# Head-pair statistics reloaded at step 6 and used from step 12, next-head loads asked for at step 6 of every other head

## The chip, the core and the metric

The kernel runs on one core of one Trainium2 chip. The core has a matrix engine (PE, with its weight loads counted apart as PEld), a vector engine (DVE), an activation engine (ACT), a general engine (POOL) and a sync engine (SP). Tiles live in SBUF, matrix results in PSUM, and larger arrays in DRAM. Copies between DRAM and SBUF are DMAs. Three engines issue them here, each into a queue of its own: SP (queue q1 in the profile), ACT (q10) and POOL (q0). All three queues are served by the same 16 DMA engines.

The metric is device time in microseconds (us) of one launch. The kernel before took 2467.77 us as the median of three runs (2467.73 to 2468.74).

## The reference

One decoder layer over 2048 tokens of width 1024, all in float32. The part that matters here is the attention of 8 heads of width 64. Every head has dilated windows; the kernel computes them as a *near* window (dilation 1) and a *far* one (dilations 4 and 16 together), and joins the two by their row maxima and softmax denominators:

```python
w = d * jnp.exp(m - jnp.max(m, axis=0, keepdims=True))
w = w / jnp.sum(w, axis=0, keepdims=True)
return jnp.sum(w[..., None] * o, axis=0)
```

Before the attention a projection makes queries, keys, values and a pooling branch; behind it come the output projection, a gated MLP with a causal convolution, a gate with per-layer embeddings, and a last RMS norm.

## The kernel before, in words

The program has three phases in a row: `phase_project` (to about 400 us in the trace), `phase_attention` (about 400 to 722 us) and `phase_rest` (the remaining 1740 us). The change touches only `phase_attention`.

**Steps.** A head's 2048 queries are cut into 16 chunks of 128. The loop `for s in range(NS + 10)` runs over 128 steps, 16 for each of 8 heads, and in each step calls the stages listed in `CFG["ord"]`, each for the step `s` minus its lag. A step computes near and far scores (lines 572, 573, 561, 562 on PE), adds the position bias and takes the row extreme (577 and 583 on DVE), exponentiates (589 and 593 on ACT), transposes the result (600, PE), copies it as a high and a low part (613 ACT, 617 DVE), and multiplies by the values (628 and 642, PE). Two of four steps end with `ev<-o` (659, ACT) and `s<-o,ev` (660, DVE), which fold a group of four chunks into the tiles `s1` (near) and `s3` (far). PE, ACT, DVE and POOL run in the order in which this loop writes their instructions (`manual_schedule`). SP is not in that list: the framework's scheduler places its DMAs, so the step at which the loop asks for a load need not be the place at which it stands in SP's queue.

**Loads.** `load_qk(h)` asks for eight tiles of a head: `qhh`, `ks`, `qll` for each half of the partitions (512 KB each), the far bias `fb` (256 KB) and the near bias `nb` (128 KB). Every tag has one buffer for even heads and one for odd heads, so a head's tiles can come in as soon as the head two before it is through. `load_v` brings value tiles (`v`, 512 KB), eight for a pair of heads. All these are DMAs of SP (line 56).

**Statistics of a pair.** Two heads form a pair; pairs are counted 0 to 3 and heads 0 to 7. When pair `pr` is done, its row extremes and denominators (`st1`, `st3`) go through five transposes (764, 767) into `sx` and `sy`. Let `d` be the step counted from the start of the next pair, so that d = 0 is the first step of heads 2, 4 and 6. The stage `M` (`mix`) then does:

- d = 1: `mix_stats_store` writes `sx` and `sy` to DRAM (`std`, `stf`; DMAs of ACT, lines 776 and 777).
- d = 4: `mix_stats_load` reads them back, turned, as `sn` and `sf` (DMAs of ACT, lines 784 and 788; 32 KB each in runs of 16 numbers, 64 bytes).
- d = 9: `mix_lift` takes the smaller extreme and the exponents (862, 865, 866 on DVE, 867 on ACT).
- d = 10: `mix_weights` makes the weights (874 to 879, DVE), and POOL writes them to DRAM (`wd`, 880).
- d = 13 + 4c for c = 0 to 3: `mix_fetch` (891, POOL) brings the weights of 512 tokens back, spread over partitions (`wb`); d = 19 + 4c: `mix_products` (901, 902, 908, POOL); d = 20 + 4c: `mix_store` (913, 914, 924, 925, POOL).

Pair 3 has no next pair and is joined in another way (`last_near`, `last_far`, `last_weights`), which the change doesn't touch.

**Waits of the DMAs.** The built program gives the DMAs of SP and ACT eight completion counters in turn (`DMAHW0` to `DMAHW7` in its listing). A DMA waits until the one before it on its counter has landed, whatever that moved. The engine that issues it waits too, and so does all that stands behind it on that engine.

Of the kernel before, what the change touches and what calls it, by code (L numbers as in the profile page):

```python
# [20 lines left out]
S = 2048  # L21
H = 8
# [18 lines left out]
V_N = V_CB + 2 * NF  # L41


CFG = {"tt": 2, "ee": 2, 'ord': [['B', 0], ['M', 0], ['N', 0], ['S', 1], ['o', 7], ['F', 0], ['h', 2], ['nm', 0], ['p', 7], ['fm', 0], ['l', 2], ['T', 1], ['V', 6], ['W', 6], ['ne', 0], ['fe', 0]], 'perm': [3, 2, 1, 0], 'fp': [[0], [1], [2], [3]], 'np': [[0, -1], [1], [2], [3]], 'm': [9, 10, 13, 4, 6, 7]}


class Shared:
# [7 lines left out]
def rdma(nc, dst, src):  # L55
    nc.sync.dma_start(fp(dst) if dst.dtype == F32R else dst, fp(src) if src.dtype == F32R else src)
# [429 lines left out]
def phase_attention(tc, g, mx, near_b, far_b):  # L486
# [5 lines left out]
    with ExitStack() as ctx:  # L492
# [42 lines left out]
        def begin(s):  # L535
# [7 lines left out]
            st = steps[s] = Shared()  # L543
            st.n = n = n - n % 4 + CFG["perm"][n % 4]
            st.t, st.pt, st.e = heads[h], pairs[h // 2], h % 2
# [5 lines left out]
            st.d1, st.d3 = st.pt.st1[:, 1, st.e, n : n + 1], st.pt.st3[:, st.r, 1, st.e, st.i : st.i + 1]  # L551
            st.tt = sb.tile([P, 768], F32, tag="tt", bufs=CFG["tt"], name="tt")
            st.ee = sb.tile([P, 768], F32, tag="ee", bufs=CFG["ee"], name="ee")

# [64 lines left out]
        def near_pv(gi, kbs, first):  # L619
            gr, q0 = groups[gi], 4 * (gi % 4)  # L620
            for kb in kbs:
                if q0 + kb < 0:
                    continue
                m0, m1 = max(0, kb), min(3, kb + 1)
                b0, b1 = 4 * m0 + kb + 1, 4 * m1 + kb + 1
                kt = q0 + kb
                for pt in (gr.h, gr.l):
                    nc.tensor.matmul(
                        gr.o[:, m0 * P : (m1 + 1) * P],
                        vals[gi // 8, "v1", kt // 4][:, kt % 4, gi // 4 % 2, :],  # L630
                        pt[:, b0 : b1 + 1 : 4, :],
                        start=first,
                        stop=False,
                        skip_group_check=True,
                    )
                    first = False

        def far_pv(gi, kbs, first):
            gr = groups[gi]
            for kb in kbs:  # L640
                for pt in (gr.h, gr.l):
                    nc.tensor.matmul(
                        gr.o[:, kb * P :],
                        vals[gi // 8, "v3", gi % 4][:, kb, gi // 4 % 2, :],
                        pt[:, 6 * kb + 2 : 18 + kb : 5, :],
                        start=first,
                        stop=False,
                        skip_group_check=True,
                    )
                    first = False  # L650
# [11 lines left out]
        def values(v):  # L662
# [4 lines left out]
            if part < 2:  # L667
                far_pv(gi, CFG["fp"][2 * part], part == 0)
            else:
                near_pv(gi, CFG["np"][2 * part - 4], part == 2)  # L670

        def values_b(v):
            gi, part = v // 4, v % 4
            if part < 2:
                far_pv(gi, CFG["fp"][2 * part + 1], False)
            else:
# [28 lines left out]
        def mix(s):  # L705
            for pr in range(NPAIR - 1):
                d = s - (pr + 1) * 2 * NQ
                if d == 1:
                    mix_stats_store(nc, g, pr, pairs[pr])
                if d == 4:  # L710
                    mix_stats_load(nc, g, mx, pr, pairs[pr])
                if d == CFG["m"][0]:
                    mix_lift(nc, g, mx, pairs[pr])
                if d == CFG["m"][1]:
                    mix_weights(nc, g, mx, pr, pairs[pr])
                for c in range(NCH):
                    if d == CFG["m"][2] + CFG["m"][3] * c:
                        mix_fetch(nc, g, mx, nc.gpsimd, pr, pairs[pr], c)
                    if d == CFG["m"][2] + CFG["m"][3] * c + CFG["m"][4]:
                        mix_products(nc, g, mx, nc.gpsimd, pairs[pr], c)  # L720
                    if d == CFG["m"][2] + CFG["m"][3] * c + CFG["m"][5]:
                        mix_store(nc, g, mx, nc.gpsimd, nc.gpsimd, pr, pairs[pr], c)()
# [5 lines left out]
        with tc.manual_schedule(engines=set(EN.values())):  # L728
            for dst, src in load_qk(0):
                rdma(nc, dst, src)  # L730
            for q in range(4):
                for which in ("v3", "v1"):
                    rdma(nc, *load_v(0, which, q))
            queue = []
            stages = {
                "F": far_scores, "N": near_scores, "fm": far_max, "nm": near_max, "fe": far_exp, "ne": near_exp,
                "T": turn, "h": high, "l": low, "V": values, "W": values_b, "S": stats, "M": mix, "o": fold, "p": folded, "B": begin
            }
            for s in range(NS + 10):
                if s < NS:  # L740
                    h, n = divmod(s, NQ)
                    if n == 1 and h + 1 < H:
                        queue += load_qk(h + 1)
                    if queue:
                        rdma(nc, *queue.pop(0))
                    for pr in range(1, NPAIR):
                        if s - 2 * NQ * (pr - 1) in V_STEPS:
                            rdma(nc, *load_v(pr, *V_STEPS[s - 2 * NQ * (pr - 1)]))
                if s == NS + 2:
                    last_far(nc, g, mx, ps_t, pairs[NPAIR - 1])  # L750
                    pieces = pairs[NPAIR - 1].pieces = last_weights(nc, mx, pairs[NPAIR - 1])
                for nm, lag in CFG["ord"]:
                    if 0 <= s - lag < NS or nm == "M":
                        stages[nm](s - lag)
                for _ in range({NS + 3: 3, NS + 4: 2, NS + 5: 1}.get(s, 0)):
                    next(pieces)
# [18 lines left out]
def mix_stats_store(nc, g, pr, pt):  # L775
    nc.scalar.dma_start(g.std[pr], pt.sx)
    nc.scalar.dma_start(g.stf[pr], pt.sy)


def mix_stats_load(nc, g, sb, pr, pt):  # L780
    q = nc.scalar
    pt.sn = sb.tile([P, 2, 2, 16], F32, tag="sn", name="sn")
    pt.sf = sb.tile([P, 2, 2, 16], F32, tag="sf", name="sf")
    q.dma_start(
        pt.sn.rearrange("p a e r -> p (a e) r"),
        g.std[pr].rearrange("(ae n) q -> ae (n q)", n=NQ).rearrange("ae (i r) -> i ae r", r=16),
    )
    q.dma_start(
        pt.sf.rearrange("p a e r -> p (a e) r"),
        g.stf[pr].rearrange("(ae n) q -> ae (n q)", n=4).rearrange("ae (i r) -> i ae r", r=16),  # L790
    )
# [66 lines left out]
def mix_lift(nc, g, sb, pt):  # L858

    sn, st3 = pt.sn, pt.sf  # L860
    lo = sb.tile([P, 2, 16], F32, tag="lo", name="lo")
    nc.vector.tensor_tensor(lo, sn[:, 0], st3[:, 0], op=ALU.min)
    pt.wts = sb.tile([P, 2, 2, 16], F32, tag="wts", name="wts")
    ex = sb.tile([P, 2, 2, 16], F32, tag="ex", name="ex")
    nc.vector.tensor_tensor(ex[:, 0], lo, sn[:, 0], op=ALU.subtract)
    nc.vector.tensor_tensor(ex[:, 1], lo, st3[:, 0], op=ALU.subtract)
    nc.scalar.activation(pt.wts, ex, AF.Exp)


def mix_weights(nc, g, sb, pr, pt):  # L870

    sn, st3, wts = pt.sn, pt.sf, pt.wts
    dn = sb.tile([P, 2, 2, 16], F32, tag="dn", name="dn")
    nc.vector.tensor_tensor(dn[:, 0], wts[:, 0], sn[:, 1], op=ALU.mult)
    nc.vector.tensor_tensor(dn[:, 1], wts[:, 1], st3[:, 1], op=ALU.mult)
    nc.vector.tensor_tensor(dn[:, 0], dn[:, 0], dn[:, 1], op=ALU.add)
    rs = sb.tile([P, 2, 16], F32, tag="rs", name="rs")
    nc.vector.reciprocal(rs, dn[:, 0])
    nc.vector.tensor_tensor(wts, wts, rs[:, None, :, :].to_broadcast([P, 2, 2, 16]), op=ALU.mult)
    nc.gpsimd.dma_start(  # L880
        g.wd[pr].rearrange("ae (i r) -> i ae r", r=16), wts.rearrange("p a e r -> p (a e) r")
    )


def mix_fetch(nc, g, sb, q, pr, pt, c, bufs=2):

    cs = slice(c * CH, (c + 1) * CH)
    wb = []
    for a in range(2):
        w = sb.tile([P, CH], F32, tag=f"wb{a}", bufs=bufs, name=f"wb{a}")  # L890
        q.dma_start(w, g.wd[pr][2 * a : 2 * a + 2, None, cs].to_broadcast([2, DH, CH]))
        wb.append(w)
    pt.__dict__.setdefault("wb", {})[c] = wb
# [1078 lines left out]
```

## Time and profile before

The profiled execution took 2463.29 us; its span from the first to the last instruction is 2461.2 us. All rows quoted from the trace come from this one execution.

| | |
|---|---|
| median of the runs | 2467.77 us (3 runs) |
| profiled execution | 2463.29 us, span 2461.2 us |
| mean granted PE clock | 0.982 |
| DMA moved | 476.06 MB, mean 193 GB/s |
| DMA of the SP queue | 396.21 MB, 51.3% of 16 engines' span |
| DMA of the ACT queue | 27.77 MB, 3.2% |

How to read it: the *timeline* lists instructions with their start, their duration, and in brackets how long the engine had been idle before and what ended that. "SPq" and "ACTq" rows are DMA issues, which cost the issuing engine little; the transfer itself lands later. The *windows* give, for a stretch of time, how long each engine was busy, the granted PE clock (1.00 is full), the mean busy share of the DMA engines and what they moved. The *chain* is the work that ended last, followed back; each piece shows its start, its length and what it was. The *DMA issues* give the size and the median time from issue to landing.

### The profile page before, as it was taken

The page shows a single profiled execution, that of the slowest core. Times are in us where ns is not written, and L with a number is a line of the kernel's source. Part 1 is how long each engine was busy: PE and PEld are TensorE (multiplying, and loading weights), DVE is VectorE, ACT ScalarE, POOL GpSimd, SP SyncE. Part 2 cuts the span into 40 slices and gives each one's busy share as a digit, 9 for nine tenths or more (in the row PEclk, how much of TensorE's full clock was granted, in tenths as well). Part 3 has the DMA queues.
Part 4 walks back from the last instruction along what each step waited for, and adds up shares of the span by engine and source line. Part 5 has one row for each costly group of instructions (what it writes and reads, how often), then busy time and mean ns, then how long its engine had stood idle before and what let it go on. Part 6 is the DMA issues. An engine that isn't in the chain of part 4 may idle for free.

```text
span 2461.2 us, 32489 instructions
## 1 busy us (share of the span) xinstructions
PE 2345.0 (95%) x11251; PEld 1969.5 (80%) x11251; DVE 1723.8 (70%) x2705; ACT 1147.7 (47%) x2055; POOL 528.9 (21%) x515
## 2 busy tenths in 40 slices
PE   8999999887878999999999999999989999999998
PEld 7888887786766887888888788788878888888888
DVE  6645427686875266999999999877766565755655
ACT  5423326786861134444445545444444444543332
POOL 3312221043350023334432366100000000000100
PEclk9999999898989999999999999999999999999999
DMA  7535348777737585456566787544378786654332
GB/s 239 175 132 184 146 156 248 174 171 175 197 124 269 187 265 194 158 192 202 192 206 212 265 278 273 201 139 139 129 251 310 222 260 203 221 176 154 126 102 90
DMA packets 250564, 476.06 MB, mean 193 GB/s; under 512 B 47744, under 2 KB 74176, under 8 KB 247328
## 3 DMA queue, kind: packets, MB, share of 16 engines
q1 hardware_dynamic: 204704, 396.21, 51.3%
q0 software_dynamic: 26048, 50.00, 6.0%
q10 hardware_dynamic: 19648, 27.77, 3.2%
q8 instruction: 88, 1.44, 0.2%
q14 instruction: 76, 0.62, 0.1%
HBM read 313.08 MB, written 160.73 MB: 193 GB/s over the span
## 4 chain that ended last, share of the span: by engine, by line
PE 73%; DVE 10%; DMA 8%; issue 3%; ACT 2%; POOL 0%; SPq 0%; DVEq 0%; POOLq 0%; ACTq 0%
PE ua L1319 15%; PE uc L1319 7%; PE dn L90 5%; PE dn L89 5%; PE dn L91 5%; PE ub L1319 4%; PE z L91 4%; PE z L89 4%; PE z L90 4%; PE o L91 2%; PE o L89 2%; PE o L90 2%; PE gp L89 2%; PE gp L90 2%; PE gp L91 2%
## 5 line engine op out<-in xcount | busy, mean ns | idle before, releaser
L89 PE MATMUL dn<-ah,wu 128*128 128x512 f32 x616 | 240.8, 391 | 5.3 <-ACT ah L84 5.3
L90 PE MATMUL dn<-al,wu 128*128 128x512 f32 x616 | 240.6, 391 | 2.1 <-DVE al L85 2.0
L91 PE MATMUL dn<-ah,wu 128*128 128x512 f32 x616 | 240.2, 390 | 0.0
L85 DVE TENSOR_TENSOR al<-ra,ah 128x512 fp32r<-128x512 f32 x154 | 105.9, 690 | 109.0 <-ACT ah L84 108.8
L89 PE MATMUL z<-hnh,wh 128*128 128x512 f32 (+1 forms) x480 | 170.1, 354 | 9.3 <-ACT hnh L252 5.8
L90 PE MATMUL z<-hnl,wh 128*128 128x512 f32 (+1 forms) x480 | 169.8, 354 | 3.6 <-DVE hnl L253 3.5
L91 PE MATMUL z<-hnh,wl 128*128 128x512 f32 (+1 forms) x480 | 169.7, 354 | 2.3 <-POOL wl L85 1.7
L84 ACT CAST ah<-ra 128x512 fp32r<-128x512 f32 x154 | 95.2, 621 | 143.1 <-PE dn L91 133.9
L110 POOL TENSOR_TENSOR pw<-ms,mhalf 128x4 f32<-128x4 f32 (+1 forms) x18 | 17.9, 995 | 636.3 <-ACT ms L108 636.3
L89 PEld LDWEIGHTS dn<-ah,wu 128*128 128x128 f32 x616 | 115.9, 188 | 30.3 <-ACT ah L84 6.2
L90 PEld LDWEIGHTS dn<-al,wu 128*128 128x128 f32 x616 | 116.0, 188 | 27.1 <-DVE al L85 3.2
L91 PEld LDWEIGHTS dn<-ah,wu 128*128 128x128 f32 x616 | 116.0, 188 | 24.2
L85 DVE TENSOR_TENSOR wu<-ru,wu 128x1024 fp32r<-128x1024 f32 x88 | 133.4, 1516 | 1.8 <-ACT wu L84 1.8
L1319 PE MATMUL uc<-a22h,wu 128*128 128x512 f32 x352 | 115.8, 390 | 2.4 <-DVE uv L1342 2.4
L1319 PE MATMUL ub<-a12h,wu 128*128 128x512 f32 x352 | 116.8, 392 | 1.2 <-ACT a12h L1375 1.2
L1319 PE MATMUL ua<-s2h,wu 128*128 128x512 f32 x352 | 116.2, 391 | 1.8 <-ACT ug L1520 1.6
L85 DVE TENSOR_TENSOR wu<-rw,wu 128x512 fp32r<-128x512 f32 x149 | 101.1, 688 | 23.5 <-ACT wu L84 23.4
L1319 PE MATMUL ua<-s1h,wu 128*128 128x512 f32 x352 | 115.6, 389 | 0.8 <-ACT ug L1546 0.8
L1319 PE MATMUL ua<-s4h,wu 128*128 128x512 f32 x352 | 115.7, 389 | 0.6 <-ACT uv L1567 0.6
L1319 PE MATMUL uc<-s3h,wu 128*128 128x512 f32 x352 | 115.6, 389 | 0.0
L1319 PE MATMUL ua<-a11h,wu 128*128 128x512 f32 x352 | 115.5, 389 | 0.0
L89 PEld LDWEIGHTS z<-hnh,wh 128*128 128x128 f32 x480 | 94.0, 196 | 21.3 <-ACT hnh L252 5.8
(334 smaller groups left out, 6713.9 us busy)
## 6 DMA issues: line engine op xcount, KB each, us to landing
ru<-in_w_up_dram SPq DMA_DIRECT2D x66, 512.0 KB, 4.2
wr<-in_w_in_dram SPq DMA_DIRECT2D x64, 256.0 KB, 4.2
rw<-in_w_down_dram SPq DMA_DIRECT2D x61, 256.0 KB, 4.0
nt<-h SPq DMA_DIRECT2D x56, 256.0 KB, 4.1
h<-h SPq DMA_DIRECT2D x56, 256.0 KB, 5.2
td<-t SPq DMA_DIRECT2D x22, 512.0 KB, 2.6
t<-td SPq DMA_DIRECT2D x22, 512.0 KB, 3.7
nt<-in_w_down_dram POOLq DMA_DIRECT2D x44, 256.0 KB, 5.1
```

The source lines that it names most:

```text
L84: nc.scalar.copy(hi, src)
L85: (low or nc.gpsimd).tensor_tensor(lo, src, fp(hi), op=ALU.subtract)
L89: nc.tensor.matmul(ps, wh, ah, start=first, stop=False, skip_group_check=again)
L90: nc.tensor.matmul(ps, wh, al, start=False, stop=False, skip_group_check=again)
L91: nc.tensor.matmul(ps, wl, ah, start=False, stop=last, skip_group_check=again)
L110: nc.gpsimd.tensor_tensor(pw[:, :nj], ms[:, :nj], g.mhalf[:, :nj], op=ALU.pow)
L1319: nc.tensor.matmul(pst, x[:, ksl], y, start=first and k == 0 and n == 0, stop=k == HK - 1 and n == 2, skip_group_check=True)
```

## The change

Two edits. The first changes the six numbers `CFG["m"]`, which are read in `mix`: lift at d = 12 (was 9), weights at d = 13 (was 10), fetch at d = 14 + 4c (was 13 + 4c), products five steps behind the fetch (were six) and store six behind it (were seven), so products and stores stay at 19 + 4c and 20 + 4c. With it the load of the statistics moves from d = 4 to d = 6. The second makes even heads (h = 0, 2, 4, 6) ask for the tiles of head h + 1 from their step 6 instead of step 1; odd heads still ask at step 1.

```diff
-... 'm': [9, 10, 13, 4, 6, 7]}
+... 'm': [12, 13, 14, 4, 5, 6]}
...
                 if d == 1:
                     mix_stats_store(nc, g, pr, pairs[pr])
-                if d == 4:
+                if d == 6:
                     mix_stats_load(nc, g, mx, pr, pairs[pr])
                 if d == CFG["m"][0]:
                     mix_lift(nc, g, mx, pairs[pr])
...
                     h, n = divmod(s, NQ)
-                    if n == 1 and h + 1 < H:
+                    if n == (1 if h % 2 else 6) and h + 1 < H:
                         queue += load_qk(h + 1)
```

In the built program ACT's two statistics loads move past two steps of its own work. These are ACT's rows at the start of head 4 (`std_116` and `stf_120` are the statistics of pair 1) before:

```order
L593 ACTIVATE ee,st_5742<-tt,st_5742 128x128 [waits DVE_49]
L784 DMA sn<-std_116 128x4x16 [waits DMAHW6_49,DMAHW2_49]
L788 DMA sf<-stf_120 128x4x16 [waits DMAHW4_49,DMAHW3_49,DMAHW0_49]
L659 COPY ev<-o 64x512 [waits PE_49]
L613 CAST pth<-tp 128x512
```

and in the changed program, from the same row on:

```order
L593 ACTIVATE ee,st_5742<-tt,st_5742 128x128 [waits DVE_49]
L659 COPY ev<-o 64x512 [waits PE_49]
L613 CAST pth<-tp 128x512
L589 ACTIVATE ee,st_5741<-tt,st_5741 128x256 [waits DVE_49,Activation_49]
L593 ACTIVATE ee,st_5742<-tt,st_5742 128x512 [waits DVE_49]
L613 CAST pth<-tp 128x256 [waits PE_49]
L589 ACTIVATE ee,st_5741<-tt,st_5741 128x256 [waits DVE_49,Activation_49]
L593 ACTIVATE ee,st_5742<-tt,st_5742 128x384 [waits DVE_49]
L784 DMA sn<-std_116 128x4x16 [waits DMAHW4_49,DMAHW2_49,DMAHW0_49]
L788 DMA sf<-stf_120 128x4x16 [waits DMAHW6_49,DMAHW3_49]
L659 COPY ev<-o 64x512 [waits PE_49]
```

`DMAHW2` and `DMAHW3` are the stores of `sx` and `sy`, which have to have landed. `DMAHW0` is the value load `v_2_2<-vf` of SP: before, `sf` stood next on its counter, now `sn` does. The other counters named were done long before.

SP's queue at the same place, before (the first number of `qhh`, `ks`, `qll`, `fb`, `nb` is a tile number; these are head 5's tiles, `v_2_...` are values of pair 2):

```order
L56 DMA v_2_2_5821<-vn 128x4x256 [waits DMAHW4_49,PE_49]
L56 DMA qll_5789<-ql_87 64x2048 [waits DMAHW5_49]
L56 DMA qhh_5788<-qh_83 64x2048 [waits DMAHW7_49]
L56 DMA v_2_3_5876<-vf 128x4x256 [waits DMAHW1_49,PE_49]
L56 DMA ks_5790<-kl_95 64x2048 [waits DMAHW2_49]
L56 DMA qll_5789<-ql_87 64x2048 [waits DMAHW3_49]
L56 DMA v_2_3_5934<-vn 128x4x256 [waits DMAHW4_49,PE_49]
L56 DMA fb_5792<-in_far_b_dram 128x512 [waits DMAHW5_49,DVE_49]
L56 DMA nb_5791<-in_near_b_dram 128x256 [waits DMAHW6_49]
```

and in the changed program:

```order
L56 DMA v_2_2_5814<-vn 128x4x256 [waits DMAHW4_49,PE_49]
L56 DMA qll_5920<-ql_87 64x2048 [waits DMAHW5_49]
L56 DMA qhh_5919<-qh_83 64x2048 [waits DMAHW6_49]
L56 DMA v_2_3_5867<-vf 128x4x256 [waits DMAHW7_49,PE_49]
L56 DMA v_2_3_5925<-vn 128x4x256 [waits DMAHW1_49,PE_49]
L56 DMA ks_5921<-kl_95 64x2048 [waits DMAHW3_49]
L56 DMA qll_5920<-ql_87 64x2048 [waits DMAHW4_49]
L56 DMA fb_5923<-in_far_b_dram 128x512 [waits DMAHW5_49,DVE_49]
L56 DMA nb_5922<-in_near_b_dram 128x256 [waits DMAHW6_49]
```

One row has moved: the last value load of the pair stands ahead of two key and query loads instead of behind them. The rest of the order is as it was, but the counters are dealt out anew, since the statistics loads now take theirs two steps later. Before, `nb` waited on the counter of `sn` (`DMAHW6`); now that counter belongs to the second `qhh`, and no load of head 5 waits for `sn` or `sf`.

More of the change, by code (lines that the diff above doesn't have):

```diff
@@ L41 @@
 V_N = V_CB + 2 * NF
-CFG = {"tt": 2, "ee": 2, 'ord': [['B', 0], ['M', 0], ['N', 0], ['S', 1], ['o', 7], ['F', 0], ['h', 2], ['nm', 0], ['p', 7], ['fm', 0], ['l', 2], ['T', 1], ['V', 6], ['W', 6], ['ne', 0], ['fe', 0]], 'perm': [3, 2, 1, 0], 'fp': [[0], [1], [2], [3]], 'np': [[0, -1], [1], [2], [3]], 'm': [9, 10, 13, 4, 6, 7]}
+CFG = {"tt": 2, "ee": 2, 'ord': [['B', 0], ['M', 0], ['N', 0], ['S', 1], ['o', 7], ['F', 0], ['h', 2], ['nm', 0], ['p', 7], ['fm', 0], ['l', 2], ['T', 1], ['V', 6], ['W', 6], ['ne', 0], ['fe', 0]], 'perm': [3, 2, 1, 0], 'fp': [[0], [1], [2], [3]], 'np': [[0, -1], [1], [2], [3]], 'm': [12, 13, 14, 4, 5, 6]}
 class Shared:
```

## The prediction

> **What bounds the kernel now.** I read the page first, then the windows, the waits and the chain inside the attention.
>
> ```profile
> span 2461.2 us, 32489 instructions
> PE 2345.0 (95%) x11251; PEld 1969.5 (80%) x11251; DVE 1723.8 (70%) x2705; ACT 1147.7 (47%) x2055; POOL 528.9 (21%) x515
> ```
>
> PE is busy for 95% of the span, but an average over three phases says little about one of them. The windows below cut the attention into heads 2 to 7, one row each, by the first `tt<-sn,nb` of a head on DVE.
>
> ```profile
> core 0: us, PE busy (x) PEld busy (x) DVE busy (x) ACT busy (x) POOL busy (x), PEclk, DMA share, GB/s
> 474.00:514.10 40.10, 32.40 (x204) 29.68 (x205) 31.47 (x97) 31.30 (x88) 4.11 (x6) 0.96 0.72 167
> 514.10:550.20 36.10, 32.68 (x212) 29.38 (x212) 30.91 (x90) 33.02 (x90) 21.23 (x21) 1.00 0.93 203
> 550.20:601.70 51.50, 35.36 (x204) 32.11 (x205) 31.47 (x98) 31.33 (x88) 16.64 (x19) 0.83 0.76 167
> 601.70:637.80 36.10, 32.67 (x212) 29.33 (x211) 30.93 (x90) 33.01 (x90) 23.28 (x25) 1.00 0.91 215
> 637.80:678.30 40.50, 32.91 (x204) 29.84 (x205) 31.61 (x98) 31.33 (x88) 11.11 (x13) 0.96 0.74 182
> ```
>
> The odd heads 3 and 5 take 36.10 us at full clock; the even heads 2, 4 and 6, in which the statistics of the pair before are handled, take 40.10, 51.50 and 40.50 for nearly the same work on each engine. A head of 16 steps without trouble is thus 36.10 us, **a step 2.26 us** (36.10/16), and the even heads lose 4.0, 15.4 and 4.4 us, together **23.8 us**. That is all that this change can win at the stage where it acts. Where it is lost, the timeline of the longest waits shows (start, duration, instruction, and in brackets the idle time before it with what ended it):
>
> ```profile
> 486.17 0.58 ACT L659 COPY ev<-o 64x512 f32<-64x512 f32 x1 [3.54 <-DMA stf<-sy]
> 487.52 0.58 PE L628 MATMUL o<-pth,v 128*128 128x256 f32 x1 [3.81 <-DVE s L660]
> 564.54 0.58 ACT L659 COPY ev<-o 64x512 f32<-64x512 f32 x1 [5.69 <-DMA v<-vn]
> 565.90 0.58 PE L628 MATMUL o<-pth,v 128*128 128x256 f32 x1 [5.96 <-DVE s L660]
> 584.51 0.19 DVE L862 TENSOR_TENSOR lo<-sn,sf 128x32 f32<-128x32 f32 x1 [7.33 <-DMA sf<-stf]
> 585.43 0.58 PE L572 MATMUL sn<-ks,qhh 128*128 128x256 f32 x1 [6.83 <-DVE st L577]
> 648.63 0.58 ACT L659 COPY ev<-o 64x512 f32<-64x512 f32 x1 [2.19 <-DMA stf<-sy]
> 662.76 0.19 DVE L862 TENSOR_TENSOR lo<-sn,sf 128x32 f32<-128x32 f32 x1 [1.60 <-DMA nb<-in_near_b_dram]
> ```
>
> There are two places in each even head. At d = 4 ACT stands before the issue of `sn` and `sf`, and with it `ev<-o` behind them, DVE's fold and PE. At d = 9 DVE stands in `mix_lift` until `sf` has landed, and PE behind it. The chain that ended last goes through the same transfers (start, length, what):
>
> ```profile
> 476.44 9.21 DMA stf<-sy
> 548.37 15.74 DMA v<-vf
> 564.13 20.36 DMA sf<-stf
> 639.74 7.79 DMA std<-sx
> 647.60 13.32 DMA sn<-std
> ```
>
> In head 2 ACT waits for the store `stf` (lands 485.65). In head 4 it waits for the value load `v<-vf`, the one before `sf` on its counter (lands 564.11), and `sf` itself then takes 20.36 us and lands at 584.49. The DMA share in these stretches is the reason that 32 KB take so long:
>
> ```profile
> 474.00:482.00 8.00, 6.61 (x45) 6.05 (x45) 6.86 (x21) 6.24 (x17) 0.00 (x0) 1.00 1.03 247
> 482.00:490.00 8.00, 4.19 (x22) 3.82 (x21) 3.62 (x11) 3.35 (x11) 0.00 (x0) 0.85 1.05 226
> 490.00:498.00 8.00, 7.32 (x47) 6.64 (x46) 6.52 (x22) 7.02 (x19) 0.00 (x0) 0.94 1.00 218
> 498.00:506.00 8.00, 7.00 (x49) 6.47 (x47) 7.37 (x30) 7.20 (x21) 1.98 (x3) 1.00 0.15 47
> ```
>
> The DMA engines are full from 474 to 498 us and nearly empty after that.
>
> **The change part by part.** *The load at d = 6, the lift at d = 12.* No instruction is added or removed. ACT comes to d = 4 at 482.63, 558.85 and 646.44 us (the `ev` rows, start less idle time). Without the two issues there it goes on and reaches d = 6 two steps later: 487.15, 563.37, 650.96. The first is behind 485.65, the third behind the 647.53 at which `std` landed, so both pass. Head 4 meets `v<-vf` at 564.11 and waits 0.7. `sf` goes out some 0.45 us behind `sn`, at about 487.6, 564.6 and 651.4. From there its own duration decides, which the DMA issues around 470 to 510, 540 to 600 and 630 to 670 us give as:
>
> ```profile
> sf<-stf ACTq DMA_DIRECT2D x1, 32.0 KB, 11.1
> sf<-stf ACTq DMA_DIRECT2D x1, 32.0 KB, 20.4
> sf<-stf ACTq DMA_DIRECT2D x1, 32.0 KB, 14.6
> ```
>
> The lift now stands eight steps behind d = 4, that is 18.1 us: at 500.7, at 577.7 (with the 0.7) and at 664.5.
>
> - Head 2: `sf` lands at 498.7, 2.0 before the lift. Nothing waits; the whole 4.0 is won.
> - Head 4: at the same duration `sf` lands at 585.0, and the lift waits 7.3 us, as long as now but three steps later. A stall of this size leaves PE slow for a while: the granted clock over the 8 us behind the last one is 0.79 (third row below), so 0.21 x 8 = 1.7 us more. Lost: 0.7 + 7.3 + 1.7 = 9.7; won: 15.4 - 9.7 = 5.7.
> - Head 6: at 14.6 us `sf` lands at 666.0 and the lift waits 1.5. But the load starts 3.3 us later than now, and the SP loads beside it ended at 664.05 (the `nb` issue below at 660.94 and its 3.1); when they end, the engines are free for it. I take that end and no wait: 4.4 won.
>
> ```profile
> 558.00:566.00 8.00, 2.04 (x15) 1.73 (x13) 2.29 (x7) 2.28 (x7) 5.01 (x6) 0.79 1.08 259
> 574.00:582.00 8.00, 4.08 (x29) 3.61 (x27) 2.83 (x7) 3.06 (x10) 0.00 (x0) 1.00 1.03 192
> 590.00:598.00 8.00, 7.81 (x47) 7.41 (x47) 5.52 (x18) 5.73 (x16) 2.42 (x3) 0.79 0.28 79
> 660.94 0.35 SPq L56 DMA_DIRECT2D nb<-in_near_b_dram  x1
> nb<-in_near_b_dram SPq DMA_DIRECT2D x1, 128.0 KB, 3.1
> 646.00:650.00 4.00, 1.55 (x12) 1.24 (x10) 1.81 (x5) 1.79 (x6) 0.00 (x0) 1.00 1.05 242
> 650.00:654.00 4.00, 4.00 (x21) 3.92 (x22) 2.57 (x8) 2.76 (x10) 0.00 (x0) 0.67 1.10 321
> ```
>
> The duration of `sf` two steps later is what the trace does not show. Its bounds are the shortest and the longest of the three. At 11.1 everywhere head 4 has no lift wait and wins 14.7: together 4.0 + 14.7 + 4.4 = 23.1. At 20.4 everywhere heads 2 and 6 wait 7.3 us each, with 1.7 for the clock: 4.0 - 9.0, 5.7 and 4.4 - 9.0, together 3.9 lost. I take each head's own duration, since the same loads surround it.
>
> The last rows also show a clock of 0.67 behind head 6's stall at d = 4, in which PE stood for about 2.5 us. The Trainium skill, in "TensorE: Matmul & The Clock Gate", Part 1, says that the clock drops after an idle window of about 3.4 us. By that rule head 6 would have lost no clock, and 0.33 x 4 = 1.3 us of the 23.8 would have another cause and stay. Here a shorter gap was enough, so I leave the 1.3 in what is won.
>
> *Weights at 13, fetch at 14 + 4c.* POOL has nothing between, and its products keep their steps. The weights leave at 500.7 + 2.3 = 503.0 or a little later, against now:
>
> ```profile
> 502.32 0.77 POOL L880 DMA_DIRECT2D wd<-wts  x1 [101.71 <-DVE st L577]
> 538.65 1.55 POOL L902 TENSOR_TENSOR m<-s,wb 128x512 f32<-128x512 f32 x1 [12.79 <-DMA wb<-wd]
> 561.08 1.51 POOL L902 TENSOR_TENSOR m<-s,wb 128x512 f32<-128x512 f32 x1 [2.77 <-DMA wb<-wd]
> ```
>
> The last of these products reads `s3` until 562.6, and DVE's fold at d = 8 of head 4 writes the same buffer. That fold comes at 564.1 + 4.5 = 568.6 by the clock of now, 4.0 earlier after the change: 564.6. If POOL's chain moves with the weights (0.7 to 1.2 later, 563.8 at most), 0.8 us are left; from there each microsecond of POOL costs one. Cost: 0, up to about 5 if the fetched weights come later still.
>
> *The loads of odd heads.* SP is not ordered by the loop, and by its rows only one value load moves, past two others. Now `nb` of head 5 waits until `sn` has landed, and lands at 586.3, while head 5 begins at 601.7; after the change the head begins at about 592 (4.0 + 5.7 earlier). I cost the edit at 0 in both directions: the 15 us of room hide it. If head 4 were to lose nothing at all, head 5 would begin at about 583 and meet these loads; then they, and not `sf`, would be the bound.
>
> **The sum** is 4.0 + 5.7 + 4.4 = **14.1 us**. The profiled execution took 2463.29 us, 2.1 more than its span, and would become 2449.2. The runs shown have their median at 2467.77, 4.5 above the profiled one; the same 14.1 less is **2453.7 us**.
>
> **The rivals.** *A, all waits go* (`sf` takes about 11 us in head 4 too): 23.1 won, 2444.7. For it: SP's second `qhh` no longer waits for the first, so its loads are further on by then. Against: the DMA engines are full there at 558 to 566 us (1.08) and still at 574 to 582 (1.03).
>
> *B, turn by turn:* `sf` keeps its duration although its neighbours end. Then head 6 waits its 1.5 and the sum is 12.6: 2455.2. The 20.36 us for 32 KB, when 11.1 were enough in head 2, speak for sharing by turns. The Trainium skill, in "DMA: Bandwidth & Descriptors", section "Queues, rings and completion order", says that each DMA engine goes round the queues that have work, a packet at a time; that is this rival's rule, and it agrees with `sf` ending long after its issue while SP's loads flow.
>
> *C, slower:* one mechanism, the statistics' transfer. It starts two steps later, so any lengthening comes straight to the lift. With one duration L for all three heads above 13.1 us, 23.1 - 5.1 - 3 x (L - 13.1) is won (three waits, three times 1.7 for the clock): nothing at 19.1, and at 22.8, the longest landing that `nb` and `fb` had in the attention, 11.1 us are lost: 2478.9. The row of that landing:
>
> ```profile
> DMA to landing us min/median/max: 3.0/15.6/22.8
> ```
>
> Against: only one of three was above 15.
>
> *D, no effect:* the second edit moves almost nothing in SP's queue. Were the d = 4 stall to come back at d = 6 (stores landing two steps later than now), nothing is won: 2467.8. Against: `stf` and `std` land 1.5 and 3.4 us before the new place.
>
> **Chances.** Forecast, with 9 to 18 us won: 0.40; B, inside the same stretch: 0.15; A: 0.18; a part of it, 5 to 9 won: 0.09; D and what else stays within 0.2% (about what a measurement of this kernel can tell from no change, 4.9 us): 0.13; C: 0.05. So faster 0.82, same 0.13, slower 0.05. The range goes from A's 2444.7, with a little room, to the 0.2% bound above: 2444.0 to 2462.8. It leaves D and C out.
>
> **What would show it.** Right: no ACT wait over 1 us before the issue of `sn` in heads 2 and 6; heads 2 and 6 at 36 to 37 us in the windows; head 4 at about 46, with one DVE wait of some 7 us before `lo<-sn,sf`; SP's issues in the order quoted. Wrong: a lift wait in head 2, an idle PE at the start of head 3, 5 or 7 that ends with `nb` or `ks`, or a fold that POOL ends. If head 1's start, which the change leaves alone, looks different, the difference is not the statistics' doing.

## The result, and the profile after

The changed kernel takes **2496.15 us** (median of 4 runs, 2488.76 to 2498.19) against 2467.75 us (median of 4 runs, 2455.66 to 2468.74) for the kernel before on the same chip: a ratio of 1.0113, 95% interval 1.009 to 1.0136, so slower by 28.4 us. The forecast was 2453.7 us. The profiled execution took 2496.5 us, 33.2 more than the one of before. First the page's head, then the windows of heads 2 to 6, with the columns of the prediction's windows:

```profile
span 2494.4 us, 32486 instructions
PE 2344.9 (94%) x11251; PEld 1969.3 (79%) x11251; DVE 1726.7 (69%) x2705; ACT 1146.8 (46%) x2055; POOL 526.4 (21%) x515
```

```profile
474.90:512.10 37.20, 31.23 (x204) 28.45 (x205) 31.37 (x97) 31.00 (x88) 3.19 (x4) 1.00 0.68 161
512.10:548.20 36.10, 32.66 (x212) 29.35 (x212) 30.90 (x90) 33.03 (x90) 10.05 (x11) 1.00 0.94 187
548.20:608.30 60.10, 33.04 (x204) 30.20 (x205) 31.40 (x97) 31.22 (x88) 25.57 (x27) 0.80 0.72 149
608.30:644.40 36.10, 32.67 (x212) 29.34 (x211) 30.89 (x90) 33.03 (x90) 9.93 (x11) 1.00 0.94 187
644.40:705.60 61.20, 33.42 (x204) 30.80 (x205) 31.40 (x97) 31.30 (x88) 25.70 (x27) 0.78 0.70 140
```

The work on each engine is that of before, and the odd heads still take 36.10 us. The even heads lose 1.1, 24.0 and 25.1 us, 50.2 together, where they lost 23.8. Head 2 came out nearly as forecast; heads 4 and 6 got a stall that was not there. The waits inside the attention (us in total, times, longest) name it; the last row is the kernel before's:

```profile
DVE s L660 <- POOL m L902: 45.0, 2, 22.9
POOL m L902 <- DMA wb<-wd: 47.6, 7, 12.1
PE o L628 <- DVE s L660: 60.2, 30, 23.2
```

```profile
POOL m L902 <- DMA wb<-wd: 20.3, 5, 12.8
```

DVE waits twice for POOL, which in turn waits for the fetched weights. In head 4 this looks so in the timeline:

```profile
587.17 1.51 POOL L902 TENSOR_TENSOR m<-s,wb 128x512 f32<-128x512 f32 x1 [5.63 <-DMA wb<-wd]
588.72 0.68 DVE L660 TENSOR_TENSOR s<-o,ev 64x512 f32<-64x512 f32 x1 [22.11 <-POOL m L902]
589.46 0.58 PE L628 MATMUL o<-pth,v 128*128 128x256 f32 x1 [22.42 <-DVE s L660]
```

It is the fold at d = 8 that writes `s3`. It comes at 566.6 (588.72 less 22.11) and has to wait until POOL's last product of the pair before has read the same buffer. That product now ends at 588.7, before at 562.6. Why it is 26 us later shows in POOL's own rows, before and then after, with the first instruction of the lift (862) and of the weights (874) on DVE and the first load of head 4 (SP) beside them:

```profile
498.58 0.17 DVE L862 TENSOR_TENSOR lo<-sn,sf 128x32 f32<-128x32 f32 x1
500.29 0.19 DVE L874 TENSOR_TENSOR dn<-wts,sn 128x32 f32<-128x32 f32 x1
504.79 2.42 POOL L891 DMA_DIRECT2D wb<-wd  x3 [1.71 <-DMA wd<-wts]
512.71 0.45 SPq L56 DMA_DIRECT2D qhh<-qh  x1
516.82 1.56 POOL L902 TENSOR_TENSOR m<-s,wb 128x512 f32<-128x512 f32 x1 [1.56 <-DMA wb<-wd]
```

```profile
501.75 0.18 DVE L862 TENSOR_TENSOR lo<-sn,sf 128x32 f32<-128x32 f32 x1
505.01 0.17 DVE L874 TENSOR_TENSOR dn<-wts,sn 128x32 f32<-128x32 f32 x1
507.02 0.77 POOL L880 DMA_DIRECT2D wd<-wts  x1 [104.51 <-DVE st L583]
509.49 2.42 POOL L891 DMA_DIRECT2D wb<-wd  x3 [1.70 <-DMA wd<-wts]
510.71 0.45 SPq L56 DMA_DIRECT2D qhh<-qh  x1
540.01 1.56 POOL L902 TENSOR_TENSOR m<-s,wb 128x512 f32<-128x512 f32 x1 [12.13 <-DMA wb<-wd]
```

The first three copies now leave 4.7 us later and the loads of head 4 start 2.0 us earlier, so the lead of the copies shrinks from 7.9 us to 1.2. Their time from issue to landing (median of the three, before, then after):

```profile
wb<-wd POOLq DMA_DIRECT2D x3, 256.0 KB, 10.7
```

```profile
wb<-wd POOLq DMA_DIRECT2D x3, 256.0 KB, 29.6
```

The windows of the same stretch show what was given away, first before, then after:

```profile
506.00:514.00 8.00, 7.19 (x51) 6.59 (x49) 7.10 (x20) 7.42 (x21) 2.03 (x4) 1.00 0.37 98
530.00:538.00 8.00, 7.15 (x48) 6.37 (x48) 7.04 (x22) 7.26 (x22) 0.00 (x0) 1.00 1.03 212
```

```profile
506.00:514.00 8.00, 6.71 (x44) 5.80 (x42) 6.86 (x23) 6.81 (x19) 3.19 (x4) 1.00 0.14 34
530.00:538.00 8.00, 7.16 (x48) 6.52 (x47) 7.11 (x21) 7.28 (x22) 0.00 (x0) 1.00 1.03 148
```

At the end of an even head the DMA engines have almost nothing to do (share 0.14 to 0.37); in the odd head behind it they are full. The copies used to run in the first stretch and now stand in the second.

Of the 33.2 us, the even heads make 26.4, and head 2 begins 0.9 us later. The remaining 5.9 lie behind the start of head 7. There PE waits 4.5 us in place of 1.5 for the copy `nr`, for which DVE waits until POOL has added up its last products of pair 2 (908). Nearly all of the other 2.9 us arises in `phase_rest`, which the change doesn't touch: its first matmul of line 854 is 30.6 us later than before (772.3 against 741.7), the end of the span 33.2. The cause is open.

### The profile page after: what moved, and what is told of

It is laid out like the page before. It is cut to its first block, busy times and chain, and to the rows that moved or that the text cites. A ratio compares the mean times of both kernels' runs of the same rounds, so it can differ in the third digit from the quotient of the medians.

```text
span 2494.4 us, 32486 instructions
## 1 busy us (share of the span) xinstructions
PE 2344.9 (94%) x11251; PEld 1969.3 (79%) x11251; DVE 1726.7 (69%) x2705; ACT 1146.8 (46%) x2055; POOL 526.4 (21%) x515
## 4 chain that ended last, share of the span: by engine, by line
PE 68%; issue 9%; DMA 9%; DVE 6%; POOL 3%; ACT 1%; SPq 0%; POOLq 0%; DVEq 0%; ACTq 0%
PE ua L1319 16%; PE uc L1319 8%; PE dn L90 5%; PE dn L89 5%; PE dn L91 5%; DMA wb<-wd 5%; PE ub L1319 4%; PE z L89 4%; PE z L91 4%; PE z L90 4%; PE o L91 2%; PE o L89 2%; PE o L90 2%; PE gp L89 2%; PE gp L91 2%
## 5 line engine op out<-in xcount | busy, mean ns | idle before, releaser
L85 DVE TENSOR_TENSOR wu<-rw,wu 128x512 fp32r<-128x512 f32 x149 | 101.0, 687 | 20.4 <-ACT wu L84 20.4
```

The costliest lines, as they stand in the source:

```text
L85: (low or nc.gpsimd).tensor_tensor(lo, src, fp(hi), op=ALU.subtract)
```

## The experiments

Two theories stood at the start. **T1**: the first edit, by its later weights, puts the fetched weights into competition with the next head's loads, and the fold waits for POOL. **T2**: the second edit fills the DMA engines in the wrong place. Each run has the kernel before timed beside it (medians 2464.8 to 2468.6 us); a ratio is the run against that, with its 95% interval.

**Each edit alone.** The first has the condition `n == 1` put back:

```diff
-                    if n == (1 if h % 2 else 6) and h + 1 < H:
+                    if n == 1 and h + 1 < H:
```

> The first edit whole (load at d = 6, lift, weights and fetch at 12, 13 and 14 + 4c), the second undone: the loads of the next head are asked for at n = 1 in every head, as before. Theory T1 (the fetched weights leave within 2 us of the next even head's loads, take 16 to 33 us in place of 8 to 11, POOL's products slip, and DVE's fold at d = 8 of heads 4 and 6 waits for POOL): the loss stays, about 2490 to 2498 us, and the waits show DVE s behind POOL m with 40 to 50 us over two waits. Rival T2 (the second edit shifts loads into the stretch around d = 6 to 9 and fills the DMA engines there): the loss goes, about 2450 to 2456 us, and no fold waits for POOL.

Measured: 2487.14 us, ratio 1.0088 (1.007 to 1.0107). The second is the kernel before with only that line of the change:

> The second edit alone: the loads of odd heads asked for at n = 6, the statistics' load and the table of steps as before. T1: no difference from before beyond 5 us, about 2463 to 2472 us; the copies of the weights land after 7 to 12 us and no fold waits for POOL. T2: slower by most of the 28 us, about 2490 us.

Measured: 2466.21 us, ratio 0.9996 (0.9979 to 1.0013). The fold's wait for POOL in the two, first edit, then second:

```profile
DVE s L660 <- POOL m L902: 36.3, 2, 20.4
```

```profile
DVE s L660 <- POOL m L902: 11.5, 1, 11.5
```

T2 falls: the first edit alone brings 21 of the 28 us, a little less than T1 expected, and the second alone none. One part of my expectation was a miss. With the second edit alone a fold does wait for POOL, 11.5 us in head 6, with weights and load where they were before. POOL's row ahead of that wait:

```profile
587.18 2.42 POOL L891 DMA_DIRECT2D wb<-wd  x3 [6.52 <-DMA wd<-wts]
```

Here POOL had to wait for its own write of `wd`, which took 6.9 us in place of 2.2. So the copies of pair 1 left only 3.5 us ahead of head 6's first load (590.69), before 9.6 us (590.69 and 600.29), and landed after a median of 20.4 us. The wait thus has the mechanism of the change; whether the second edit brings it each time, one execution can't tell. Whether the second edit adds to the loss of the first (2487 against 2496 us) isn't settled; the two intervals overlap.

**No transfer of the fetched weights.** The tiles are filled by POOL, so the product's weights are constants:

```diff
-        q.dma_start(w, g.wd[pr][2 * a : 2 * a + 2, None, cs].to_broadcast([2, DH, CH]))
+        nc.gpsimd.memset(w, 0.25)
```

> The change with the transfers of the fetched weights left out: POOL fills the tiles wb with a constant instead (the broadcast of the softmax weights over the rows is left out). T1: POOL's products stand at their own steps, the two stalls between d = 8 and d = 9 of heads 4 and 6 vanish, and what the load at d = 6 gives is won: 2443 to 2456 us, with a lift wait for sf in head 4 of up to 10 us. T2 (the stalls come from the head loads and sf, not from POOL's chain): the stalls of over 20 us stay, now on another wait, 2485 to 2498 us.

Measured: 2448.7 us, ratio 0.9933 (0.9915 to 0.995). Windows of heads 4 and 6, the lift's wait for `sf` in the whole attention, and the landing of `sf` in head 4:

```profile
546.98:583.73 36.75, 31.27 (x204) 28.51 (x205) 31.45 (x97) 31.01 (x88) 5.58 (x8) 1.00 0.70 162
619.86:656.50 36.64, 31.28 (x204) 28.51 (x205) 31.35 (x97) 30.99 (x88) 5.58 (x8) 1.00 0.62 150
```

```profile
DVE lo L862 <- DMA sf<-stf: 0.4, 1, 0.4
```

```profile
sf<-stf ACTq DMA_DIRECT2D x1, 32.0 KB, 13.2
```

Both stalls are gone, and with them nearly every other loss of these heads (0.65 and 0.54 us above 36.10 remain). So the 45.0 us hang on these copies, and `sf` too lands sooner without them (13.2 us against 25.4 in the change).

**Late weights on the kernel before.** Load at d = 4, lift at 9, second edit absent:

```diff
-... 'm': [9, 10, 13, 4, 6, 7]}
+... 'm': [9, 13, 14, 4, 5, 6]}
```

> The kernel before with one thing of the change: the weights at d = 13 in place of 10 (fetch at 14 + 4c; POOL's order, products and stores are the same). The load stays at d = 4 and the lift at d = 9, loads of odd heads as before. By the before profile wd would leave at about 509 us and the copies at 511.5, about 1 us ahead of the loads of head 4 at 512.7. T1: the copies take 16 to 33 us as in the change, the folds at d = 8 of heads 4 and 6 wait for POOL some 15 to 23 us each, and the time is 2485 to 2510 us. Rival T3 (the moved load of the statistics is needed for the loss, since without ACT's stall the whole of head 2 to 4 runs closer together): under 2475 us.

Measured: 2489.18 us, ratio 1.0103 (1.0082 to 1.0125). POOL's copies, head 4's first load, the landing, and the fold's wait:

```profile
512.63 2.42 POOL L891 DMA_DIRECT2D wb<-wd  x3 [1.70 <-DMA wd<-wts]
513.84 0.45 SPq L56 DMA_DIRECT2D qhh<-qh  x1
```

```profile
wb<-wd POOLq DMA_DIRECT2D x3, 256.0 KB, 30.3
```

```profile
DVE s L660 <- POOL m L902: 23.7, 2, 18.0
```

The later weights, with the fetch that follows them, give nearly the whole loss (24.4 us), without the moved load; T3 falls. The folds wait less than I expected (23.7 us, not 30 to 46). I take it that the stall at d = 4, which stays here, hides a part; no run separates that.

**Steps between.** All of lift, weights and fetch one step earlier than the change (`[11, 12, 13, 4, 6, 7]`):

> The change with lift, weights and fetch each one step earlier (11, 12 and 13 + 4c; products and stores at their steps, load at d = 6, second edit kept). The copies of the weights then leave some 2.3 us earlier beside the same loads of the next head, about where they left before. T1: most of the new wait goes: the fold behind POOL keeps under 10 us of its 45, heads 4 and 6 win most of what the load at d = 6 gives, and the time is 2450 to 2462 us, with a lift wait of 0 to 2 us in head 2 and up to 10 in head 4. T2: as the change, about 2490 to 2498 us.

Measured: 2472.8 us, ratio 1.0029 (1.0016 to 1.0042). Of the change's 28.4 us some 7 remain. The first copies land after 17.8 us (median of three), and the folds keep 29.1 of 45.0 us, more than the 10 I expected: one step is not enough lead.

```profile
wb<-wd POOLq DMA_DIRECT2D x3, 256.0 KB, 17.8
```

```profile
DVE s L660 <- POOL m L902: 29.1, 2, 18.2
```

And with the load at d = 5 and `[10, 11, 12, 4, 7, 8]`:

> The change with the load at d = 5, lift at 10, weights at 11 and fetch at 12 + 4c (products and stores at their steps, second edit kept). wd then leaves at about 501 us in head 2, as in the kernel before. T1: the copies land after 8 to 12 us, the fold behind POOL keeps 0 to 12 us over both heads, the lift waits 0 to 2 us in head 2 and up to 8 in head 4: 2448 to 2464 us. Rival: the lift waits take what POOL gives (3 to 10 us in each head), 2464 to 2475 us.

Measured: 2469.51 us, ratio 1.0011 (0.9987 to 1.0034). No fold waits for POOL any more. But the lift waits for `sf`, and at d = 5 ACT stands again before the issue of the loads: in head 4 for a load of SP (second row: `pth` stands behind the two issues), in head 6 for 6.8 us whose end the profile doesn't name.

```profile
DVE lo L862 <- DMA sf<-stf: 7.4, 3, 3.8
```

```profile
ACT pth L613 <- DMA ks<-kh: 5.1, 1, 5.1
```

The rival's time was right. Its lift waits were smaller than it has them (7.4 us in all); the waits of ACT take the rest of what POOL gives back.

**Another queue for the copies.** Chunks 0 and 1 issued by SP ahead of the loads:

```diff
-                    if d == CFG["m"][2] + CFG["m"][3] * c:
-                        mix_fetch(nc, g, mx, nc.gpsimd, pr, pairs[pr], c)
+                    if d == CFG["m"][2] + (CFG["m"][3] * c if c > 1 else 0):
+                        mix_fetch(nc, g, mx, nc.gpsimd if c > 1 else nc.sync, pr, pairs[pr], c)
```

> The change, with the copies of chunks 0 and 1 issued by SP (all four at d = 14, ahead of the next head's loads in SP's order) in place of POOL; chunks 2 and 3 stay with POOL at 22 and 26. T1, in the form that the first copies lose against the loads because they stand in another queue: the four copies land in under 12 us, products of chunks 0 and 1 run at their steps, and the folds at d = 8 wait under 10 us together: 2448 to 2462 us. Rival: the copies of chunks 2 and 3 still land after 20 us or more beside the loads and POOL ends as late as now, 2480 us or more; or the loads behind the copies come late and the next head waits for ks or qll.

Measured: 2488.75 us, ratio 1.0097 (1.0079 to 1.0115). The same with lift, weights and fetch a step earlier:

> The edit of the run before with lift, weights and the first fetch one step earlier as well (11, 12, 13; chunks 2 and 3 fetched at 21 and 25; products and stores at their steps). T1: wd leaves some 2.3 us earlier, the copies land by about 512 us before the loads of the next head begin to flow, POOL is never late: no fold waits for POOL over 3 us, 2445 to 2455 us. Rival as in the run before: 2465 us or more.

Measured: 2486.64 us, ratio 1.0085 (1.0062 to 1.0109). Both miss T1's time; what came is the rival's second form, late loads behind the copies. In the first of them SP's issues, a PE row at the start of head 4, and the window of head 3 show where the wait went:

```profile
512.40 9.59 SPq L891 DMA_DIRECT2D wb<-wd  x4
522.09 5.06 SPq L56 DMA_DIRECT2D qhh<-qh  x1
527.25 0.55 SPq L56 DMA_DIRECT2D ks<-kh  x1
```

```profile
562.25 0.55 PE L572 MATMUL sn<-ks,qhh 128*128 128x256 f32 x1 [12.77 <-DMA ks<-kl]
```

```profile
515.25:568.37 53.12, 34.08 (x212) 29.93 (x211) 30.95 (x91) 33.03 (x90) 20.25 (x20) 0.85 0.66 158
```

No fold waits for POOL now, as T1 has it. But the copies hold SP's queue: `ks` goes out at 527.25 (in the change at 511.25), and PE waits for it. The odd heads lose what the even heads win. It is not that the DMA engines had no room. From 512 to 528 us their share is 0.15 here (first row), in the change 0.95 (second row):

```profile
512.00:528.00 16.00, 14.54 (x97) 13.47 (x97) 13.95 (x42) 14.89 (x43) 3.89 (x3) 1.00 0.15 47
```

```profile
512.00:528.00 16.00, 14.52 (x95) 13.20 (x95) 13.62 (x40) 15.08 (x41) 2.09 (x2) 1.00 0.95 181
```

SP spends 9.59 us on the four issues and 5.06 on the next one, where its issues of head 4's loads in the change take 0.43 to 1.13 us each. So an issue isn't always cheap for the engine that makes it. What holds SP there the profile doesn't name.

**Can both be beaten?** Four versions ask for the first copies in the same step as the weights. Each half of the fetched weights gets three buffers, paid by one buffer less for each half of the split. The first is the kernel before with fetch at 10 + 4c:

```diff
-        hi, low = (sb.tile([P, CH], F32R, tag=f"wb{y}", bufs=2, name=f"w{y}")[:8] for y in range(2))
+        hi, low = (sb.tile([P, CH], F32R, tag=f"wb{y}", bufs=3, name=f"w{y}")[:8] for y in range(2))
...
-def mix_fetch(nc, g, sb, q, pr, pt, c, bufs=2):
+def mix_fetch(nc, g, sb, q, pr, pt, c, bufs=3):
...
-    hi = sb.tile([P, CH], F32R, tag="ah", bufs=3, name="ah")
-    lo = sb.tile([P, CH], F32R, tag="al", bufs=3, name="al")
+    hi = sb.tile([P, CH], F32R, tag="ah", bufs=2, name="ah")
+    lo = sb.tile([P, CH], F32R, tag="al", bufs=2, name="al")
...
-... 'm': [9, 10, 13, 4, 6, 7]}
+... 'm': [9, 10, 10, 4, 9, 10]}
```

> The kernel before with three buffers for each half of the fetched weights (two for each half of the split, to pay for them) and fetch at 10 + 4c in place of 13 + 4c (products at 19 + 4c, stores at 20 + 4c as before), so that six of the eight copies are asked for right behind the weights. T1, in the form that the copies are cheap before the loads of the next head and dear beside them: the first six copies have landed or nearly so by 520 us, POOL's last product of a pair ends earlier than the 562.6 us of before, no fold waits for POOL; the stalls at d = 4 and in the lift stay, so 2455 to 2468 us, no clear difference. Rival: copies in flight slow each other and the loads, and the time is 2475 us or more.

Measured: 2462.46 us, ratio 0.9973 (0.9959 to 0.9987). POOL's last product of pair 0 and the next three copies:

```profile
510.77 0.78 POOL L891 DMA_DIRECT2D wb<-wd  x1 [5.77 <-issue]
512.61 1.58 POOL L891 DMA_DIRECT2D wb<-wd  x2 [1.06 <-issue]
...
556.36 1.55 POOL L902 TENSOR_TENSOR m<-s,wb 128x512 f32<-128x512 f32 x1
```

The product ends at 557.9 in place of 562.6, and no fold waits for POOL. But only three copies, not six, were through by 520: the fourth went out when the first had landed, and it and the next two then took 23 to 28 us beside the loads. The other three are built on the change and keep a later load of the statistics. Load at d = 6 with `[11, 12, 12, 3, 7, 8]`:

> The change with the same three buffers, lift at 11, weights at 12, fetch at 12 + 3c, products at 19 + 3c, stores at 20 + 3c (load at d = 6, second edit kept). T1: wd leaves as in the run one step earlier, six copies are asked for at once, some of them still beside the next head's loads; but the last product now stands three steps (6.8 us) earlier, so the folds at d = 8 wait under 10 us together in place of 29: 2450 to 2464 us. Rival (the DMA engines are full in the odd heads whatever the order, so what POOL does not wait for the loads will): 2468 us or more, with waits for ks, qll or nb at the starts of heads.

Measured: 2468.53 us, ratio 1.0006 (0.9988 to 1.0023); the folds wait 9.1 us, as T1 has it, the lift 5.9, and the time is the rival's. Load at d = 5 with `[10, 11, 11, 3, 8, 9]`:

> As the run before, all of it one step earlier: load at d = 5, lift at 10, weights at 11, fetch at 11 + 3c, products at 19 + 3c, stores at 20 + 3c. T1: copies before the loads, no fold waits for POOL; lift waits of 2 to 4 us in each even head as in the run with the load at 5: 2450 to 2462 us, below the kernel before. Rival as in the run before: 2468 us or more.

Measured: 2460.99 us, ratio 0.9972 (0.9952 to 0.9992), though its profiled execution was its slowest (2472.43 us), with 20.1 us of lift waits, more than the 2 to 4 us a head that I expected. Last, that version with the lift at 11:

> As the run with the load at d = 5 and three buffers, with the lift at 11 in place of 10, in the same step as the weights (fetch at 11 + 3c, products at 19 + 3c, stores at 20 + 3c as there). There the lift waited 20.1 us for sf over the three even heads, up to 7.9 in one; one step more takes up to 2.3 us from each. T1: no fold waits for POOL over 3 us, lift waits under 15 us together, 2453 to 2463 us, below the kernel before. Rival: what the lift no longer waits, the folds or the heads' starts wait (copies 0 to 2 us closer to the loads of the next head): 2464 us or more, no difference from before.

Measured: 2462.3 us, ratio 0.9982 (0.9966 to 0.9998), with 3.4 us of lift waits and no fold behind POOL. Three of the four thus lie 0.2 to 0.3% below the kernel before, the change 1.1% above it. Their intervals end at 0.9987, 0.9992 and 0.9998, so the last of them at least may be chance; which of them is best can't be told.

## Why the prediction was wrong

- **The step that failed is "Weights at 13, fetch at 14 + 4c".** It saw the right place: the fold at d = 8, the buffer `s3`, 0.8 us of margin, "from there each microsecond of POOL costs one", and a fold that POOL ends is in its list of what would show it wrong. It mis-sized the term: "0, up to about 5", measured 45.0. Two things were wrong in it. The weights did not leave at 503.0 but at 507.02. The lift came at 501.75 in place of 500.7; the step from there to the weights took 3.3 us (to 505.01) in place of 2.26, so steps are not equal; and the 2.0 us from the first instruction of the weights to the issue of `wd` were left out, though before has them too (500.29 to 502.32). And the copies' landing was kept at its old duration. The rows of the SP loads were read for what the loads do to `sf`, and never laid beside the time at which `wb` would leave. The late weights by themselves, on the kernel before, cost 2489 us; without the copies the change takes 2448.7.
- **The stalls at d = 4** went as forecast: no row of the waits after has ACT behind a store or a value load there. Head 2 took 37.2 us against "36 to 37".
- **The lift's wait of 7.3 us in head 4** did not come. In the change the fold's stall covers it (`sf` lands 25.4 us after its issue, but DVE stands at d = 8 until 588.7). Without the copies `sf` took 13.2 us and the lift waited 0.4 in all. So the duration taken from before, 20.4 us, belonged to that moment's traffic and not to head 4. Without the copies head 7 begins 21.8 us earlier than before (656.50 against 678.30), near the 23.1 that rival A wins; but of the whole time 17.3 us are won (2448.7 against 2466.03 of the kernel before beside it), between the forecast's 14.1 and A's 23.1. As the copies' own traffic is gone in that run too, it doesn't show the moved load's gain by itself.
- **The second edit at 0** was right by itself: ratio 0.9996. Its part beside the first edit is open.
- **Rival C** ended on the right side for a wrong reason. It has the statistics' transfer lengthen. That came true in heads 4 and 6 (`sf` took 25.4 and 27.0 us), but no lift waited for it, since DVE stood at the fold until `sf` had landed. What cost the time was the transfer of the weights made from these statistics. No rival had POOL's copies in it.

## What to carry to other kernels

When a step is moved, lay the issue times of its DMAs beside those of every other queue, as they will be after the change, and price each transfer by the company it will have. A gap in the DMA share can be worth as much as a gap on an engine: here the end of head 2 carried three copies in 8 to 11 us each, and the same copies, issued 4.7 us later, took 16 to 33. Where a margin is under 1 us and the cost beyond it is one for one, the uncertainty of the producer's time is the price, not the margin.

## What the runs showed of the hardware

Three copies of 256 KB took a median of 10.7 us ahead of the next head's loads and 29.6 us beside them. The median went with the lead of the first copy over head 4's first load: 10.7 us at a lead of 7.9 us (before), 10.6 at 6.3 (load at d = 5, weights at 11), 17.8 at 3.7 (one step earlier), 29.6 at 1.2 (the change), 30.3 at 1.2 (late weights on the kernel before).

From 520 to 530 us of the change the DMA engines were full (share 1.03) and had work of both queues. Their packets there (packets, MB, share of 16 engines; q1 is SP, q0 is POOL):

```profile
q1 hardware_dynamic: 272, 1.80, 91.1%
q0 software_dynamic: 146, 0.21, 11.6%
```

SP's loads had nearly twice the packets of the copies and, with a mean of 6.6 KB against 1.4 KB, over eight times their bytes. The Trainium skill, in "DMA: Bandwidth & Descriptors", section "Queues, rings and completion order", says that each DMA engine goes round the queues that have work, a packet at a time. These counts are not one to one, and the trace doesn't tell which engine had work of which queue at a time, so no run here shows that rule or refutes it. The Trainium skill, in "SBUF — State Buffer", section "SBUF: two separate sides", warns of another cause, that some DVE operations keep POOL from writing the descriptors of its DMAs. DVE's busy time does not tell the two cases apart here: 7.10 of 8 us while the copies were fast and 7.11 of 8 while they were slow.

The fourth copy that POOL issues for a pair left 0.4 us behind the landing of the first in every trace that has one, with two buffers and with three; what sets that limit wasn't tried.
